# Log-sigmoid of the gates spread over 128 partitions, sums of x built on POOL from high and low parts

## The chip, the cores and the metric

The kernel runs on one core of one Trainium2 chip. Its time is the device time of one execution in microseconds (us). A core has a matrix engine (PE, with its weight load PEld), a vector engine (DVE), a scalar engine (ACT), a fourth engine for general work (POOL), a sequencer that issues transfers (SP), and DMA engines that move data between the chip's main memory and the on-chip memory, SBUF. PE writes its results to PSUM, from which DVE and ACT read. In the trace's names, `SPq` and `POOLq` are the transfers that SP and POOL issue.

## The reference

One inference step of a one-layer decoder: 512 prompt tokens and 8 x 4 sample tokens, 544 rows in all, each of 2048 numbers. All rows go through one large input projection; the mLSTM branch and the sliding-window attention branch work on its columns, and two further projections and an output projection follow. What matters here is the start:

```python
u = jnp.einsum('btd,dc->btc', x, w_in)      # 2048 inputs, 18,952 columns
...
q_m, k_m, v_m, o_m, z_m, q_a, k_a, v_a, z_a, g_m, g_a, i_pre, f_pre = parts
...
ig = (i_pre + b_igate).astype(jnp.float32)
lf = jax.nn.log_sigmoid((f_pre + b_fgate).astype(jnp.float32))
```

There are 4 heads, so `i_pre` and `f_pre` have 4 columns each. The mLSTM takes running sums of `lf` and running maxima of `ig` less those sums along the tokens of each head. Everything else of the mLSTM (decays, weights, stabilisers) is computed from these. The products are held in near-f32 accuracy.

## The kernel before

**Splitting.** PE multiplies a reduced-precision type (`fp32r` in the trace). Each f32 operand is therefore split into a high part (ACT: a copy that rounds; for weights L200, CAST in the trace) and a low part (DVE: the original less the high part; for weights L201). A product is three matmuls: high by high, high by low, low by high. `hilo` (L243 on ACT, L244 on DVE) does this for data.

**The x stage** (L287 to L346). x is loaded in columns, PE transposes it in blocks of 128 into a PSUM tile `pt` (`sm` in the trace), and for each of 16 blocks `hilo` writes high and low parts. For blocks 0 to 7 the first 272 rows of x go to `a11` and the rest to `a21`; blocks 8 to 15 go to `xk2`. ACT also copies the transposed x in f32 into `n2r` (L327) and `s1r` (L328, L338). From these, sums and differences are made: DVE subtracts in `s1r` (L332, L342), POOL adds `n3r = n2r + s1r` in four chunks of 128 x 544 (L346) when block 7 is in place, POOL subtracts in `n2r` later (`x_sums`), and high and low parts of the sums (`n3`, `s1`, `n2`, `s4`) are written by ACT and DVE (L565 for `n3l`, L244 for the others).

**The products.** The first two 128-column blocks are plain products, with the gate products (`gates_half`) between. After that, pairs of 128-column blocks go through `paired`: seven half-size products per pair in place of eight, from sums of the weights' quarters and sums of x's quarters (one level of a Strassen-type scheme). `prepare` makes the weights' sums, on DVE (L644) or, where an operand accumulates in place, as a transfer that adds (L642, issued by POOL's queue), and splits them. `half_product` (L664 and L666) issues the matmuls. `gather` combines the results: ACT evacuates (L682), POOL subtracts (L683), DVE does the rest (L685 to L693). The gathered blocks and other results pass through a pool of three buffers, `ev`.

**What runs beside.** The vector work of the gates, of the keys and of the values is written as generators (`gates`, `attn_values`, `attn_keys`, `x_sums`) that are advanced one step at a time: the products call `tick()`, and each `yield` ends a step. So the place of an instruction in DVE's order is set by the number of `yield`s ahead of it, together with a scheduler that respects priorities (`high_priority`). On each engine the order is fixed when the program is built.

`gates` first joins the four PSUM pieces of the gate products to `ig` and `fg`, of 4 partitions (the heads) by 544 tokens (L403 to L410). Then come, all on 4 partitions: the absolute value and the exponential on ACT (L414, L415), and on DVE `2 + e`, a reciprocal (L420), two multiplications (L424, L425), a polynomial (L427 to L432, with seven coefficients) and the joining of the minimum (L433, L434): `lf = min(f, 0) - log(1 + exp(-|f|))`, by a series. Fills (L438 to L440, L445 to L447) make the reset masks for two scans (L441: the running sum; L451: the running maximum). Rows of 4 x 544 live in a pool `t544` of 12 buffers.

`attn_values` copies 32 sample rows of the values into a buffer `vs` taken from `ev` (L533, L535) and stores it. `attn_keys` (L548 to L551) copies keys to a buffer `kr` taken from `ev`, and stores them in two transfers.

SP issues the weight loads (512 KB each), the stores of results and the small loads in program order.

Of the kernel before, what the change touches and what calls it, by code (L numbers as in the profile page):

```python
# [17 lines left out]
AF = mybir.ActivationFunctionType  # L18
ALU = mybir.AluOpType

D = 2048
SEQ = 512
NB = 8
NTS = 4
NS = NB * NTS
T = SEQ + NS
# [42 lines left out]
def build(tc, nc, i, o, dbg=None):  # L69
    es = ExitStack()  # L70
    with es:
        _build(tc, nc, i, o, es)


def _build(tc, nc, i, o, es):
# [3 lines left out]
    def pool(stack, name, bufs, space=None, side=None):  # L79
        kw = {"space": space} if space is not None else {}  # L80
        if space is None:
            kw["side"] = side or "right"
            kw["reuse_waits"] = "tile"
        return stack.enter_context(tc.tile_pool(name=name, bufs=bufs, **kw))

    y_p, y_s, C_p, n_p, m_p, kb_p, vb_p, C_s, n_s, m_s, kb_s, vb_s = o
    V, A, G, PE = nc.vector, nc.scalar, nc.gpsimd, nc.tensor
# [13 lines left out]
    def nm(s):  # L101
        count[0] += 1
        return f"{s}_{count[0]}"

    def sm():
        return psB.tile([128, 512], F32, tag="sm", name=nm("sm"))

    def ev(n=T):
        return evp.tile([128, n], F32, tag="ev", name=nm("ev"))

    def r32(ap):
        return ap.bitcast(F32)
# [4 lines left out]
    def blk(ap, n=4):  # L117
        return ap.rearrange("p (b x) -> p b x", b=n)
# [123 lines left out]
    def hilo(src, hi, lo, eng=None):  # L242
        A.copy(hi, src)  # L243
        (eng or V).tensor_tensor(out=lo, in0=src, in1=r32(hi), op=ALU.subtract)  # L244
# [10 lines left out]
    HT = T // 2  # L255

    def quad(p, s):
        return [p.tile([128, 8, HT], F32R, tag="act", name=nm(s + n)) for n in "hl"]

    a11, a21 = quad(act, "a11"), quad(act, "a21")  # L260
# [16 lines left out]
    esG = ExitStack()  # L277
# [5 lines left out]
    n2r = tx.tile([128, 8, HT], F32, name="n2r")[:]  # L283
    s1r, n3r = (act2.tile([128, 8, HT], F32, tag="act", name=nm("r"))[:] for _ in range(2))

    def two_k(ch):
        return slice(ch * 2, ch * 2 + 2)  # L287
# [11 lines left out]
    for c0, n in ((0, 256), (256, 256), (512, 512), (1024, 512), (1536, 512)):  # L299
        if c0 < 1536:  # L300
            t_ = xr.tile([128, 4, n], F32, tag=f"x{n}", name=nm("xr"))[:]
        else:
            t_ = act2.tile([128, 8, HT], F32, tag="act", name=nm("xr"))[:].rearrange("p a b -> p (a b)")
            t_ = blk(t_[:, 0:4 * n])
# [10 lines left out]
    for g in range(8):  # L315
        for q in range(2):
            k = g * 2 + q
            pt = sm()
            for t in range(4):
                PE.transpose(pt[:, t * 128:t * 128 + 128], xt[k][:, t], ident)  # L320
            if k == 2:
                for c in range(4):
                    PE.transpose(pxs[:, c * 128:c * 128 + 128], xs[:, c], ident)
            if k < 8:
                hilo(pt[:, 0:HT], a11[0][:, k], a11[1][:, k])
                hilo(pt[:, HT:SEQ], a21[0][:, k, 0:SEQ - HT], a21[1][:, k, 0:SEQ - HT])
                A.copy(n2r[:, k], pt[:, 0:HT])  # L327
                A.copy(s1r[:, k, 0:SEQ - HT], pt[:, HT:SEQ])  # L328
            else:
                hilo(pt[:], xk2[0][k // 4 - 2][:, k % 4, 0:SEQ], xk2[1][k // 4 - 2][:, k % 4, 0:SEQ])  # L330
                c = (slice(None), k - 8, slice(0, SEQ - HT))
                state["x_end"] = V.tensor_tensor(out=s1r[c], in0=pt[:, HT:SEQ], in1=s1r[c], op=ALU.subtract)  # L332
        if g % 2:
            k4 = slice((g // 2) * 4, (g // 2) * 4 + 4)
            src = pxs[:].rearrange("p (c q t) -> p q c t", c=4, q=4)[:, g // 2]
            if g < 4:
                hilo(src, *(a21[p][:, k4, SEQ - HT:HT] for p in range(2)))
                A.copy(s1r[:, k4, SEQ - HT:HT], src)  # L338
            else:
                hilo(src, *(xk2[p][g // 2 - 2][:, :, SEQ:T] for p in range(2)))  # L340
                c = (slice(None), slice(k4.start - 8, k4.stop - 8), slice(SEQ - HT, HT))
                V.tensor_tensor(out=s1r[c], in0=src, in1=s1r[c], op=ALU.subtract)  # L342
        if g == 3:
            for ch in range(4):
                ks_ = two_k(ch)
                G.tensor_tensor(out=n3r[:, ks_], in0=n2r[:, ks_], in1=s1r[:, ks_], op=ALU.add)  # L346
    esXr.close()
    t544 = pool(esG, "t544", 12)

    def t5(dt=F32, n=T):  # L350
        return t544.tile([128, n], dt, tag="t544", name=nm("t"))
# [41 lines left out]
    def gates(ps):  # L393
        def row(n=T):
            return t5(n=n)[:4]
# [5 lines left out]
            return ap.unsqueeze(2).to_broadcast([4, NB, NTS])  # L401

        ig, fg, u, u2 = row(), row(), row(), row()  # L403
        for p_, (u_, v_), (ig_, fg_) in zip(ps, *(
                [(a[:, c:c + HT], b[:, c:c + HT]) for c in (0, HT)] for a, b in ((u, u2), (ig, fg)))):
            A.copy(u_, p_[64:68, :HT])
            A.copy(v_, p_[96:100, :HT])
            V.scalar_tensor_tensor(ig_, p_[0:4, :HT], bi[:, 0:1], u_, op0=ALU.add, op1=ALU.add)
            V.scalar_tensor_tensor(fg_, p_[32:36, :HT], 0.0, v_, op0=ALU.add, op1=ALU.add)
        V.tensor_scalar(fg, fg, bi[:, 1:2], None, op0=ALU.add)  # L410
        yield
        e_ = row()
        A.activation(e_, fg, AF.Abs)
        A.activation(e_, e_, AF.Exp, scale=-1.0)  # L414
        yield  # L415
        yield

        dd, s, s2, p, lf = row(), u, u2, row(), row()
        V.tensor_scalar(dd, e_, 2.0, None, op0=ALU.add)
        V.reciprocal(dd, dd)  # L420
        yield
        yield
        yield
        V.tensor_tensor(out=s, in0=e_, in1=dd, op=ALU.mult)  # L424
        V.tensor_tensor(out=s2, in0=s, in1=s, op=ALU.mult)  # L425
        yield
        V.tensor_scalar(p, s2, 1.0 / 15, None, op0=ALU.mult)  # L427
        for c in (13, 11, 9, 7, 5, 3):
            V.scalar_tensor_tensor(p, p, 1.0 / c, s2, op0=ALU.add, op1=ALU.mult)
            if c % 4 == 1:  # L430
                yield
        V.scalar_tensor_tensor(p, p, 1.0, s, op0=ALU.add, op1=ALU.mult)  # L432
        V.tensor_scalar(lf, fg, 0.0, None, op0=ALU.min)  # L433
        V.scalar_tensor_tensor(lf, p, -2.0, lf, op0=ALU.mult, op1=ALU.add)  # L434
        yield

        rst, c = s, s2
        V.memset(rst, 1.0)  # L438
        V.memset(rst[:, 0:SEQ:128], 0.0)
        V.memset(rst[:, SEQ:T:NTS], 0.0)  # L440
        V.tensor_tensor_scan(c, rst, lf, 0.0, ALU.mult, ALU.add)  # L441
        ap, d0 = lf, row()
        V.tensor_tensor(out=ap, in0=ig, in1=c, op=ALU.subtract)
        yield
        V.memset(d0, 0.0)  # L445
        V.tensor_copy(d0[:, 128:SEQ:128], c[:, 127:SEQ - 1:128])
        V.memset(d0[:, SEQ:T:NTS], NEG)  # L447
        am, M = p, fg
# [58 lines left out]
        for src, rep, dst, m in ((T2, reps[0], colT2, 3), (T1, reps[1], colT1, 4)):  # L507
            pt, pt2 = sm(), sm()
# [15 lines left out]
    def attn_values(kk, vt):  # L524

        for _ in range(3):
            yield
        pt, pt2 = sm(), sm()
        for b in range(4):
            PE.transpose(pt[:, b * 128:b * 128 + 128], vt[:, b * 128:b * 128 + 128], ident)  # L530
        PE.transpose(pt2[:32, 0:128], vt[:, SEQ:T], ident)
        cs = slice(kk * 128, kk * 128 + 128)
        vr, vs = ev(512), ev(128)  # L533
        A.copy(vr[:], pt[:])
        V.tensor_copy(vs[:32], pt2[:32, 0:128])  # L535
        nc.sync.dma_start(d_vr[0:SEQ, cs].rearrange("(b p) c -> p b c", p=128), blk(vr[:]))
        nc.sync.dma_start(d_vr[SEQ:T, cs], vs[:32])
        nc.sync.dma_start(vb_p[0].rearrange("t k d -> t (k d)")[:, cs], vr[:, 384:512])
# [777 lines left out]
    for part, h in ((oz, 0), (oz, 1), (vkq, 2), (vkq, 3), (oz, 2), (oz, 3)):  # L1316
        work += part(h)
    work += merge_gates[7:]
    gates_ = gates(gates_ps)
    next(gates_)  # L1320
    spawn(gates_)
# [6 lines left out]
    def branch(src, p, tmp, ahead=()):  # L1328

        hs, los = act_tiles(p, "bh"), act_tiles(p, "bl")  # L1330

        def steps():
            for k in range(KT):
                if k < len(ahead):
                    st = ahead[k]
                else:
                    st = tmp(k)
                    nc.sync.dma_start(st[:], src[k])
                hilo(st[:], hs[k // 4][:, k % 4], los[k // 4][:, k % 4])
                yield  # L1340
        return (hs, los), whole(hs), whole(los), steps()

    _, bah, bal, g_ = branch(d_bra, act, lambda k: ev(), ahead)
# [12 lines left out]
    t544 = pool(esA, "t512", 18)  # L1356
# [289 lines left out]
    d0 = pool(esD, "d0", 1, side="left")  # L1646
# [248 lines left out]
```

## Time and profile before

| | |
|---|---|
| median of 3 runs | 2493.77 us (2491.63 to 2494.89) |
| profiled execution: its own time | 2497.55 us |
| its span (first to last instruction) | 2495.7 us |
| mean granted TensorE clock | 0.995 |
| PE busy in the span | 2453.8 us (98%) |
| DVE, ACT, POOL busy | 73%, 50%, 15% |
| costliest groups off PE | L201 on DVE 778.9 us, L200 on ACT 661.9 us, L644 on DVE 304.5 us |
| POOL's largest group | L683, 82 instructions, 124.8 us, 1522 ns each |

The profiled execution is one run, with the profiler on; the three timed runs have none. The traced times are read against the span of that execution, and differences worked out from them are then set against the median. A row of the timeline gives the start and the duration in us, the engine, the line of the kernel, the operation, output and inputs with partitions x elements, and in brackets the idle time just before with what ended it. Neighbouring instructions can overlap a little, since the start of one is put down before the end of the one ahead. A row of the groups gives busy time and mean duration in ns, then the idle time before the group.

### The profile page before, as it was taken

How to read it: one execution, taken by the hardware profiler on the slowest of the kernel's cores; microseconds unless marked ns; L12 is line 12 of the kernel's file. 1: busy time of each engine (PE TensorE's matmuls, PEld its weight loads, DVE VectorE, ACT ScalarE, POOL GpSimd, SP SyncE). 2: the span in 40 equal slices, each digit the busy share in tenths (PEclk: the TensorE clock that was granted, in tenths of full speed). 3: DMA queues.
4: the chain of work that ended last, by engine and by line, in shares of the span. 5: the costliest groups of instructions: out<-in, count | busy, mean ns of one | idle time of the engine just before them, and what ended most of it. 6: DMA issues, size and time to landing. Idle time of an engine off the chain costs nothing. (4 is left out here: it accounts for less than half of the span.)

```text
span 2495.7 us, 48772 instructions
## 1 busy us (share of the span) xinstructions
PE 2453.8 (98%) x19542; PEld 2394.0 (96%) x19542; DVE 1817.8 (73%) x2785; ACT 1244.1 (50%) x2033; POOL 373.1 (15%) x376
## 2 busy tenths in 40 slices
PE   8999999999999999999999999999999999999997
PEld 8999999999999999989999999999999999999997
DVE  7867677677677677777878788878855654666667
ACT  6457677667667665433433444444633333334431
POOL 2111121121111111121021121210000000110111
PEclk9999999999999999999999999999999999999999
DMA  6677666656666655468678677677755546788776
GB/s 166 154 185 187 150 151 159 158 144 163 153 152 156 151 128 151 106 204 243 205 216 243 167 232 240 188 225 226 251 171 172 189 149 205 198 229 258 213 220 190
DMA packets 557172, 464.71 MB, mean 186 GB/s; under 512 B 45328, under 2 KB 454080, under 8 KB 556688
## 3 DMA queue, kind: packets, MB, share of 16 engines
q1 hardware_dynamic: 540048, 402.07, 54.4%
q0 software_dynamic: 15696, 57.15, 11.8%
q8 instruction: 154, 2.52, 0.4%
q10 hardware_dynamic: 1200, 2.36, 0.3%
q14 instruction: 74, 0.61, 0.1%
HBM read 319.06 MB, written 96.31 MB: 166 GB/s over the span
## 5 line engine op out<-in xcount | busy, mean ns | idle before, releaser
L200 ACT CAST wh<-raw 128x1024 fp32r<-128x1024 f32 x632 | 661.9, 1048 | 814.6 <-PE bank L664 663.8
L201 DVE TENSOR_TENSOR wl<-raw,wh 128x1024 fp32r<-128x1024 f32 x632 | 778.9, 1234 | 222.7 <-ACT wh L200 203.4
L664 PE MATMUL bank<-xk,wh 128*128 128x272 f32 x2336 | 325.0, 290 | 0.9 <-DVE ev L689 0.9
L644 DVE TENSOR_TENSOR raw<-raw,raw 128x1024 f32<-128x1024 f32 x238 | 304.5, 1280 | 17.3 <-DMA raw<-in_w_in 8.2
L664 PEld LDWEIGHTS bank<-xk,wh 128*128 128x128 f32 x2336 | 304.3, 189 | 4.2 <-issue 2.6
L683 POOL TENSOR_TENSOR ev<-p,ev 128x272 f32<-128x272 f32 x82 | 124.8, 1522 | 674.1 <-ACT ev L682 613.7
L666 PE MATMUL bank<-xk,wl 128*128 128x272 f32 x1168 | 172.4, 288 | 0.8 <-DVE wl L201 0.8
L664 PE MATMUL bank<-s1h,wh 128*128 128x272 f32 x656 | 169.1, 291 | 0.2 <-ACT wh L200 0.2
L664 PE MATMUL bank<-n3h,wh 128*128 128x272 f32 x656 | 169.1, 289 | 0.0
L664 PE MATMUL bank<-n2h,wh 128*128 128x272 f32 x656 | 168.2, 289 | 0.6 <-ACT wh L200 0.6
L664 PE MATMUL bank<-s4h,wh 128*128 128x272 f32 x656 | 168.3, 290 | 0.1
L664 PE MATMUL bank<-n3l,wh 128*128 128x272 f32 x656 | 167.9, 287 | 0.0
L664 PE MATMUL bank<-n2l,wh 128*128 128x272 f32 x656 | 167.5, 287 | 0.0
L664 PE MATMUL bank<-s1l,wh 128*128 128x272 f32 x656 | 167.2, 287 | 0.0
L664 PE MATMUL bank<-s4l,wh 128*128 128x272 f32 x656 | 167.0, 287 | 0.0
L666 PEld LDWEIGHTS bank<-xk,wl 128*128 128x128 f32 x1168 | 156.6, 188 | 1.1 <-DVE wl L201 1.0
L664 PE MATMUL bank<-a11h,wh 128*128 128x272 f32 x584 | 150.8, 290 | 2.6 <-ACT wh L200 2.5
L209 PE MATMUL bank<-bh,wl 128*128 128x272 f32 x704 | 148.5, 291 | 4.7 <-DVE wl L201 4.7
L664 PE MATMUL bank<-a11l,wh 128*128 128x272 f32 x584 | 149.6, 289 | 0.0
L209 PE MATMUL bank<-bh,wh 128*128 128x272 f32 x704 | 148.8, 290 | 0.0
L209 PE MATMUL bank<-bl,wh 128*128 128x272 f32 x704 | 148.6, 290 | 0.0
L664 PEld LDWEIGHTS bank<-n3h,wh 128*128 128x128 f32 x656 | 123.3, 188 | 1.9 <-issue 1.4
(488 smaller groups left out, 5515.4 us busy)
## 6 DMA issues: line engine op xcount, KB each, us to landing
raw<-in_w_in SPq DMA_DIRECT2D x296, 512.0 KB
raw<-raw POOLq DMA_DIRECT2D x90, 512.0 KB, 5.0
C<-in_state_mlstm_C SPq DMA_DIRECT2D x32, 1024.0 KB
out<-C SPq DMA_DIRECT2D x64, 512.0 KB
raw<-in_w_proj_a SPq DMA_DIRECT2D x32, 512.0 KB
raw<-in_w_proj_m SPq DMA_DIRECT2D x32, 512.0 KB
raw<-in_w_out SPq DMA_DIRECT2D x32, 512.0 KB
d_v<-ev SPq DMA_DIRECT2D x16, 272.0 KB
```

The source lines that it names most:

```text
L200: A.copy(wh[:, k:k + n], raw[:, k:k + n])
L201: V.tensor_tensor(out=wl[:, k:k + n], in0=raw[:, k:k + n], in1=r32(wh[:, k:k + n]), op=ALU.subtract)
L209: PE.matmul(ps[f][:, :w], a[:, kk], b(k, c, w), start=(k == 0 and n == 0), stop=(k == 15 and n == 2))
L644: V.tensor_tensor(out=w[out][:], in0=w[a][:], in1=w[b][:], op=ALU.add)
L664: PE.matmul(ps, wh[:, k], x(p, k), start=(first and k == 0 and p == 0), stop=False, skip_group_check=True)
L666: state["end"] = PE.matmul(ps, wl[:, k], x(0, k), start=False, stop=(k == 7), skip_group_check=True)
L683: G.tensor_tensor(out=c22, in0=p1, in1=c11, op=ALU.subtract)
```

## The change

Three parts.

1. **Sums of x.** ACT no longer copies the transposed x into `n2r` and `s1r` (18 copies fall away). POOL adds high and low parts instead: when blocks 0 to 3, and again when blocks 4 to 7, are in place, two chunks of 128 x 544 each for `s1r` (from `a21`) and for `n2r` (from `a11`). That is eight POOL additions more, ahead of the four for `n3r`.
2. **Log-sigmoid.** `fg` is moved by a transfer from 4 partitions of 544 to 128 partitions of 17 (`f7`, a slice of one new buffer `w7`); ACT's two steps and DVE's fourteen run on 128 x 17, and a second transfer brings the result back to `lf`, 4 x 544. Both transfers are issued by SP. The same arithmetic is done. The large fills of the scans' masks (`rst`, `d0`) go to POOL; one strided copy and one fill for the second scan stay on DVE. There are fewer `yield`s. `t544` has 13 buffers.
3. **`vs`** comes from `t544` in place of `ev`.

```diff
--- before.py
+++ after.py
@@ -324,8 +324,6 @@
             if k < 8:
                 hilo(pt[:, 0:HT], a11[0][:, k], a11[1][:, k])
                 hilo(pt[:, HT:SEQ], a21[0][:, k, 0:SEQ - HT], a21[1][:, k, 0:SEQ - HT])
-                A.copy(n2r[:, k], pt[:, 0:HT])
-                A.copy(s1r[:, k, 0:SEQ - HT], pt[:, HT:SEQ])
             else:
                 hilo(pt[:], xk2[0][k // 4 - 2][:, k % 4, 0:SEQ], xk2[1][k // 4 - 2][:, k % 4, 0:SEQ])
                 c = (slice(None), k - 8, slice(0, SEQ - HT))
@@ -335,7 +333,10 @@
             src = pxs[:].rearrange("p (c q t) -> p q c t", c=4, q=4)[:, g // 2]
             if g < 4:
                 hilo(src, *(a21[p][:, k4, SEQ - HT:HT] for p in range(2)))
-                A.copy(s1r[:, k4, SEQ - HT:HT], src)
+                for t_, (h_, l_) in ((s1r, a21), (n2r, a11)):
+                    for ch in (g - 1, g):
+                        ks_ = two_k(ch)
+                        G.tensor_tensor(out=t_[:, ks_], in0=r32(h_[:, ks_]), in1=r32(l_[:, ks_]), op=ALU.add)
             else:
                 hilo(src, *(xk2[p][g // 2 - 2][:, :, SEQ:T] for p in range(2)))
                 c = (slice(None), slice(k4.start - 8, k4.stop - 8), slice(SEQ - HT, HT))
@@ -345,7 +346,7 @@
                 ks_ = two_k(ch)
                 G.tensor_tensor(out=n3r[:, ks_], in0=n2r[:, ks_], in1=s1r[:, ks_], op=ALU.add)
     esXr.close()
-    t544 = pool(esG, "t544", 12)
+    t544 = pool(esG, "t544", 13)
 
     def t5(dt=F32, n=T):
         return t544.tile([128, n], dt, tag="t544", name=nm("t"))
@@ -401,6 +402,7 @@
             return ap.unsqueeze(2).to_broadcast([4, NB, NTS])
 
         ig, fg, u, u2 = row(), row(), row(), row()
+        w7 = t5(n=6 * 17)
         for p_, (u_, v_), (ig_, fg_) in zip(ps, *(
                 [(a[:, c:c + HT], b[:, c:c + HT]) for c in (0, HT)] for a, b in ((u, u2), (ig, fg)))):
             A.copy(u_, p_[64:68, :HT])
@@ -408,41 +410,38 @@
             V.scalar_tensor_tensor(ig_, p_[0:4, :HT], bi[:, 0:1], u_, op0=ALU.add, op1=ALU.add)
             V.scalar_tensor_tensor(fg_, p_[32:36, :HT], 0.0, v_, op0=ALU.add, op1=ALU.add)
         V.tensor_scalar(fg, fg, bi[:, 1:2], None, op0=ALU.add)
-        yield
-        e_ = row()
-        A.activation(e_, fg, AF.Abs)
-        A.activation(e_, e_, AF.Exp, scale=-1.0)
-        yield
-        yield
-
-        dd, s, s2, p, lf = row(), u, u2, row(), row()
-        V.tensor_scalar(dd, e_, 2.0, None, op0=ALU.add)
-        V.reciprocal(dd, dd)
-        yield
-        yield
-        yield
-        V.tensor_tensor(out=s, in0=e_, in1=dd, op=ALU.mult)
-        V.tensor_tensor(out=s2, in0=s, in1=s, op=ALU.mult)
-        yield
-        V.tensor_scalar(p, s2, 1.0 / 15, None, op0=ALU.mult)
-        for c in (13, 11, 9, 7, 5, 3):
-            V.scalar_tensor_tensor(p, p, 1.0 / c, s2, op0=ALU.add, op1=ALU.mult)
-            if c % 4 == 1:
-                yield
-        V.scalar_tensor_tensor(p, p, 1.0, s, op0=ALU.add, op1=ALU.mult)
-        V.tensor_scalar(lf, fg, 0.0, None, op0=ALU.min)
-        V.scalar_tensor_tensor(lf, p, -2.0, lf, op0=ALU.mult, op1=ALU.add)
-        yield
-
-        rst, c = s, s2
-        V.memset(rst, 1.0)
-        V.memset(rst[:, 0:SEQ:128], 0.0)
-        V.memset(rst[:, SEQ:T:NTS], 0.0)
+        e_, dd, p, lf, d0 = (row() for _ in range(5))
+        rst, c = u, u2
+        G.memset(d0, 0.0)
+        f7, e7, d7, s7, q7, p7 = (w7[:, n * 17:n * 17 + 17] for n in range(6))
+        nc.sync.dma_start(f7, fg)
+        yield
+        yield
+        A.activation(e7, f7, AF.Abs)
+        A.activation(e7, e7, AF.Exp, scale=-1.0)
+        yield
+
+        V.tensor_scalar(d7, e7, 2.0, None, op0=ALU.add)
+        V.reciprocal(d7, d7)
+        V.tensor_tensor(out=s7, in0=e7, in1=d7, op=ALU.mult)
+        V.tensor_tensor(out=q7, in0=s7, in1=s7, op=ALU.mult)
+        V.tensor_scalar(p7, q7, 1.0 / 15, None, op0=ALU.mult)
+        for n in (13, 11, 9, 7, 5, 3):
+            V.scalar_tensor_tensor(p7, p7, 1.0 / n, q7, op0=ALU.add, op1=ALU.mult)
+        V.scalar_tensor_tensor(p7, p7, 1.0, s7, op0=ALU.add, op1=ALU.mult)
+        V.tensor_scalar(f7, f7, 0.0, None, op0=ALU.min)
+        V.scalar_tensor_tensor(f7, p7, -2.0, f7, op0=ALU.mult, op1=ALU.add)
+        nc.sync.dma_start(lf, f7)
+        G.memset(rst, 1.0)
+        G.memset(rst[:, 0:SEQ:128], 0.0)
+        G.memset(rst[:, SEQ:T:NTS], 0.0)
+        yield
+        yield
+
         V.tensor_tensor_scan(c, rst, lf, 0.0, ALU.mult, ALU.add)
-        ap, d0 = lf, row()
+        ap = lf
         V.tensor_tensor(out=ap, in0=ig, in1=c, op=ALU.subtract)
         yield
-        V.memset(d0, 0.0)
         V.tensor_copy(d0[:, 128:SEQ:128], c[:, 127:SEQ - 1:128])
         V.memset(d0[:, SEQ:T:NTS], NEG)
         am, M = p, fg
@@ -530,7 +529,7 @@
             PE.transpose(pt[:, b * 128:b * 128 + 128], vt[:, b * 128:b * 128 + 128], ident)
         PE.transpose(pt2[:32, 0:128], vt[:, SEQ:T], ident)
         cs = slice(kk * 128, kk * 128 + 128)
-        vr, vs = ev(512), ev(128)
+        vr, vs = ev(512), t5(n=128)
         A.copy(vr[:], pt[:])
         V.tensor_copy(vs[:32], pt2[:32, 0:128])
         nc.sync.dma_start(d_vr[0:SEQ, cs].rearrange("(b p) c -> p b c", p=128), blk(vr[:]))
```

## The prediction

> **What bounds the kernel now.** I read the page first, then stretches of 25 us, then the PE, DVE, ACT, POOL and SP timelines of the first 105 us. The built programs order every engine's instructions alike behind about 150 us, so only the start can differ.
>
> ```profile
> PE 2453.8 (98%) x19542; PEld 2394.0 (96%) x19542; DVE 1817.8 (73%) x2785; ACT 1244.1 (50%) x2033; POOL 373.1 (15%) x376
> ```
> ```profile
> 25.00:50.00 25.00, 23.20 (x183) 22.53 (x184) 22.42 (x40) 15.25 (x36) 10.77 (x9) 1.00 0.42 96
> 50.00:75.00 25.00, 24.20 (x194) 23.97 (x193) 24.02 (x30) 13.52 (x22) 6.74 (x5) 1.00 0.51 111
> 75.00:100.00 25.00, 23.00 (x178) 22.10 (x177) 21.80 (x37) 8.29 (x10) 3.30 (x3) 1.00 0.70 182
> 100.00:125.00 25.00, 23.31 (x185) 23.00 (x183) 19.72 (x36) 13.59 (x19) 2.43 (x3) 1.00 0.70 163
> ...
> 150.00:175.00 25.00, 25.00 (x201) 25.00 (x201) 15.88 (x19) 13.24 (x18) 3.11 (x3) 1.00 0.81 196
> ```
> Columns of the stretches are the length, then PE, weight load, DVE, ACT and POOL busy. PE is the bound. From 150 us it never rests (201 matmuls in 25 us, 0.125 us each); before that it rests while DVE is all but full, 24.02 of 25 us. Most that the change can win is PE rest ahead of 105 us. The rests that matter, with the start of the first weight pair's products (57.79) for a mark:
>
> ```profile
> 57.79 0.29 PE L664 MATMUL bank<-a11h,wh 128*128 128x272 f32 x1
> ...
> 69.77 1.27 PE L666 MATMUL bank<-xk,wl 128*128 128x272 f32 x8 [0.80 <-DVE wl L201]
> ...
> 78.42 0.39 PE L664 MATMUL bank<-a11h,wh 128*128 128x272 f32 x1 [0.84 <-ACT wh L200]
> ...
> 81.55 2.27 PE L664 MATMUL bank<-xk,wh 128*128 128x272 f32 x16 [0.86 <-DVE ev L689]
> ...
> 85.96 0.39 PE L664 MATMUL bank<-s1h,wh 128*128 128x272 f32 x1 [0.16 <-ACT wh L200]
> ...
> 103.78 0.39 PE L664 MATMUL bank<-a11h,wh 128*128 128x272 f32 x1 [1.69 <-ACT wh L200]
> ```
> They add up to 0.80 + 0.84 + 0.86 + 0.16 + 1.69 = 4.35 us. A gain over 0.2% (5 us, about what a measurement of this kernel can tell from no change) therefore needs the stage of the x transposes, ahead of 57.79, as well.
>
> **The log-sigmoid.** The old chain works on 4 partitions of 544 elements, so each step costs its full length:
>
> ```profile
> L429 DVE SCALAR_TENSOR_TENSOR t<-t,t 4x544 f32<-4x544 f32 x6 | 4.2, 695 | 0.0
> L420 DVE RECIPROCAL t<-t 4x544 f32<-4x544 f32 x1 | 3.5, 3541 | 0.0
> ...
> L425 DVE TENSOR_TENSOR t<-t 4x544 f32<-4x544 f32 x1 | 0.7, 706 | 0.0
> ...
> L438 DVE MEMSET t<- 4x544 f32 x1 | 0.5, 512 | 0.1
> ...
> L535 DVE COPY ev<-sm 32x128 f32<-32x128 f32 x1 | 0.3, 279 | 2.8 <-DMA out<-ev 2.8
> ...
> L450 DVE TENSOR_TENSOR t<-t,m0t 4x8 f32<-4x8 f32 x1 | 0.2, 153 | 0.0
> ```
> Removed from DVE: the reciprocal 3.5, six polynomial steps 4.2, four more two-input steps like L425 (L424, L432, L434) 4 x 0.7 = 2.8, the long fills L438 and L445 1.0, and three one-input steps I put at 0.4 each, 1.2: 12.7 us. In their place are fourteen steps on 128 partitions of 17. Nothing in the trace has that shape; nearest is the 0.15 us row of 8 elements, so 14 x 0.15 = 2.1 us (above by the 32-column steps, not much more). DVE wins some 10.6 us. Keeping the small value copy out of the `ev` buffers also removes the 2.8 us for which DVE stood behind a store. That DVE time is worth only what PE waited for, and what comes late next is a chain that runs through POOL and transfers:
>
> ```profile
> 66.48 3.85 POOL L683 TENSOR_TENSOR ev<-p,ev 128x272 f32<-128x272 f32 x1 [10.39 <-ACT ev L682]
> 70.29 0.86 POOL L642 DMA_DIRECT2D raw<-raw  x1
> ...
> 94.61 1.64 POOL L683 TENSOR_TENSOR ev<-p,ev 128x272 f32<-128x272 f32 x1 [8.72 <-DMA out<-ev]
> 96.21 0.86 POOL L642 DMA_DIRECT2D raw<-raw  x1
> ```
> ```profile
> 76.38 1.99 ACT L200 CAST wh<-raw 128x1024 fp32r<-128x1024 f32 x2 [4.17 <-DVE t L447]
> ...
> 101.74 1.99 ACT L200 CAST wh<-raw 128x1024 fp32r<-128x1024 f32 x2 [5.05 <-DMA raw<-raw]
> ```
> ```profile
> 90.33 0.27 DVE L548 COPY ev<-sm 128x128 f32<-128x128 f32 x1
> ```
> ```profile
> 91.06 0.38 SPq L551 DMA_DIRECT2D d_ks<-ev  x1
> ```
> ```profile
> 61.03 0.49 DVE L410 TENSOR_SCALAR t<-t,bi 4x544 f32<-4x544 f32 x1
> ```
> Read it forward: POOL's subtraction (L683), POOL's accumulating transfer at 70.29, the cast at 76.38 (6.1 us on), DVE's work up to the key copy at 90.33, its store from 91.06 on, POOL's next subtraction that reuses that buffer at 94.61 (3.2 us after the store was issued at 91.44), the transfer at 96.21, the two casts at 101.74, PE at 103.78. In the changed program these links remain:
> (i) Start. The gates are complete at 61.5 (L410 at 61.03). The transfer out is issued by SP in 0.4, lands after 3.2 (from the 91.44 to 94.61 above; the other bound is 6.1, the accumulating transfer), two ACT steps take 0.4, then ACT's queued cast 1.0 and evacuation 0.4, POOL 1.64: 68.6 instead of 70.29, 1.7 us earlier. POOL's 3.85 falls to the 1.64 of its later row, since the 3.5 us reciprocal, on DVE at the same time, is gone. ACT stands on this transfer with the casts of the later products queued behind; PE wants the first of them some 12 us after it starts the pair, which covers it up to a landing of about 7 us.
> (ii) DVE from the cast to the key copy: the second scan and its sums now stand there instead of the polynomial, while the 2.8 us wait is gone. I add the instructions in the new order, 13.3 us behind the first cast's 1.0, against the 13.95 between 76.38 and 90.33 that held both casts: 0.4 later by that count, or 0.6 earlier when the cast is taken inside; I take 0.6 earlier and keep both. The transfer back lands during the weight subtraction ahead of the scan, so costs nothing; without that cover it costs what it exceeds 1.2 us.
> (iii) PE's first product behind the last transfer is now that of the first cast, not the second: 1.0 us earlier.
> Sum: -(1.7 + 0.6 + 1.0) = -3.3 us. PE alone could come 4.35 earlier, so the chain decides; a wait of about 1 us stays near 100 us. SP's issue of the outward transfer also holds back the next weight load, which waits until 62.68 for DVE anyway.
>
> ```profile
> 62.68 0.38 SPq L635 DMA_DIRECT2D raw<-in_w_in  x1
> ```
>
> **The sums of x.** ACT loses eighteen copies; POOL takes eight additions more.
>
> ```profile
> L327 ACT COPY n2r<-sm 128x272 f32<-128x272 f32 x8 | 3.4, 427 | 0.2 <-DVE a21l L244 0.2
> L328 ACT COPY r<-sm 128x240 f32<-128x240 f32 x8 | 3.3, 410 | 0.0
> ```
> ```profile
> L244 DVE TENSOR_TENSOR xk<-sm,xk 128x512 fp32r<-128x512 f32 x6 | 4.1, 680 | 0.8 <-ACT xk L243 0.8
> ...
> L244 DVE TENSOR_TENSOR a11l<-sm,a11h 128x272 fp32r<-128x272 f32 x7 | 3.0, 437 | 3.5 <-ACT a11h L243 3.5
> ```
> ```profile
> L346 POOL TENSOR_TENSOR r<-n2r,r x4: 1338/1354/1842, 14.9 to 28.9; 128x544 f32<-128x544 f32 x4
> ```
> The copies stood in front of the casts that DVE waited for, 3.5 + 0.8 = 4.3 us; I take all of it back. Against it: DVE steps with two inputs in SBUF stop while a POOL addition runs.
>
> ```profile
> 18.82 0.72 DVE L565 SCALAR_TENSOR_TENSOR n3l<-r,n3h 128x544 fp32r<-128x544 f32 x1
> ...
> 23.70 1.16 DVE L565 SCALAR_TENSOR_TENSOR n3l<-r,n3h 128x544 fp32r<-128x544 f32 x1
> ...
> 29.68 1.96 DVE L385 TENSOR_TENSOR wga<-graw,wga 128x32 fp32r<-128x32 f32 x2
> ...
> 40.22 3.79 DVE L244 TENSOR_TENSOR s1l<-r,s1h 128x544 fp32r<-128x544 f32 x4
> ...
> 47.29 0.29 DVE L385 TENSOR_TENSOR wga<-graw,wga 128x32 fp32r<-128x32 f32 x2
> ```
> ```profile
> 28.92 1.36 POOL L346 TENSOR_TENSOR r<-n2r,r 128x544 f32<-128x544 f32 x1
> ```
> The two `wga` steps take 1.96 beside additions and 0.29 without; with 0.4 + 0.2 on two of the four n3l steps and 1.1 on the s1l steps, DVE pays 3.4 us over these ten steps now, 0.34 each, with eight additions. With sixteen, back to back from about 13 us, twelve such steps fall among them; at twice the density w = 0.68 each, which is also half an addition, that is 8.2 us. Net: 8.2 - 3.4 - 4.3 = +0.5 us, which PE pays at the end of the transposes, since in the new order it has no gate products left to fill in there. The Trainium skill's "SBUF — State Buffer", section "Who interferes with whom", speaks against the change here: a DVE instruction with two SBUF inputs and a GpSimd instruction that reads SBUF exclude each other for the whole instruction. Read at its worst, every step would wait one addition whole, 12 x 1.35 - 7.7 = +8.5, and the sum would be +5.2 instead of -2.8; the 1.96 beside the 28.92 POOL row shows the exclusion, and the 0.72 row that not every step meets it.
>
> ```profile
> 28.00 0.97 POOL L379 MEMSET wgb<- 128x1024 f32 x1
> ```
> The fills on POOL go into its idle time (15% busy), at most 1 us each by the 0.97 row, ahead of buffers that DVE needs later. Bounded below by no gain, above by 1 us.
>
> **Sum.** -3.3 + 0.5 = -2.8 us against the profiled 2497.55 (its span 2495.7 and 1.85 around it): 2494.7. The median of the runs shown is 2493.77, 3.8 below the profiled one; I forecast on that scale, 2493.77 - 2.8 = 2491.0.
>
> **Rivals.** With w as the mean wait of the twelve steps, the total is -3.3 - 7.7 + 12w.
> *Faster by more than 0.2%*: w under 0.50. For it: the 0.34 of today, and DVE finds POOL waiting for it as often. Against it: twice the additions. At 0.34 the sum is -6.9, 2486.9. Chance 0.38, since ACT's relief may also shorten PE's smaller gaps that I left alone.
> *Slower*: POOL becomes the bound of the x stage. Its sixteen additions and two fills (the 0.97 row) take 16 x 1.35 + 2 x 0.97 = 23.5 us, and whatever DVE blocks is added; the sums, the second gate weights and the high and low parts all queue behind. It decides above w = 1.33, a whole addition. With additions stretched towards the 1.84 of the longest row, w = 1.5 gives +7.0, 2500.8. For it: the pair at 29.68 came close to 0.84 each. Chance 0.14.
> *The transfers take the place of the arithmetic*: the first lands after 6.1 instead of 3.2, moving link (i) by 2.9: +0.1, 2493.9, no measurable change. Both transfers queue on SP behind 512 KB loads, which speaks for it; chance 0.18, of which 0.06 for landings so late that ACT's casts hold PE (slower).
> The forecast itself, w between 0.50 and 1.33 with prompt transfers: 0.30.
>
> **How the numbers follow.** Within 0.2%: 0.30 + 0.12 = 0.42. Faster: 0.38. Slower: 0.14 + 0.06 = 0.20. The likeliest case's own range is 2488.8 to 2498.8; the range for all runs from w = 0.2 (-8.6, 2485) to the slower rival's near part, 2500.
>
> **What would show it.** Right: no PE rest between 58 and 95 us, one of 1 to 2 us near 100 us behind an ACT cast; POOL at its subtraction in about 1.6 us; DVE's 17-element steps near 0.15; n3l, wga and wl steps over 1.2 us beside POOL additions between 13 and 42 us, and the start of the first pair's products near 58. Wrong: that start before 55 or after 62, an ACT idle above 3 us ahead of the absolute value, a scan waiting for the transfer back, or any difference that opens behind 150 us.

## The result, and the profile after

Over 22 runs of each kernel the changed one takes 2486.77 us (median; 2482.05 to 2494.10) and the one before 2490.85 us. The ratio is 0.9982, with a 95% interval of 0.9976 to 0.9988: 4.5 us faster, between 3.0 and 6.0. That is 0.18%, just on the near side of the 0.2% drawn as a line in the prediction. (The median of before over 22 runs lies 2.9 us under that of the first three.)

The profiled execution took 2484.96 us, its span is 2483.2 us. Its engines, as in the first section of the page:

```profile
PE 2447.4 (99%) x19542; PEld 2390.9 (96%) x19542; DVE 1811.9 (73%) x2781; ACT 1238.8 (50%) x2015; POOL 385.1 (16%) x388
```

The stretches of 25 us (length, then PE, weight load, DVE, ACT, POOL busy, then the granted clock):

```profile
25.00:50.00 25.00, 22.72 (x179) 21.95 (x178) 22.74 (x39) 14.29 (x32) 15.87 (x13) 1.00 0.47 116
50.00:75.00 25.00, 25.00 (x203) 24.99 (x202) 20.90 (x39) 14.24 (x23) 3.90 (x6) 1.00 0.60 142
75.00:100.00 25.00, 23.38 (x183) 22.72 (x183) 23.30 (x44) 11.93 (x18) 4.16 (x5) 1.00 0.68 169
100.00:125.00 25.00, 25.00 (x203) 24.85 (x202) 17.03 (x23) 10.16 (x14) 3.95 (x4) 1.00 0.86 216
```

PE no longer rests from 50 to 75 and from 100 to 125 us, where it had 24.20 and 23.31 of 25. Its rests, from the timeline, with the start of the first pair's products:

```profile
22.52 0.63 PE L320 MATMUL sm<-cc,xr 128*128 128x128 f32 x4 [2.72 <-DVE a21l L244]
...
46.19 0.48 PE L391 MATMUL bank<-xk,wga 128*128 128x272 f32 x2 [2.28 <-DVE wga L386]
...
56.26 0.29 PE L663 MATMUL bank<-a11h,wh 128*128 128x272 f32 x1
...
80.85 1.27 PE L665 MATMUL bank<-a11h,wl 128*128 128x272 f32 x8 [0.84 <-DVE wl L201]
...
90.83 1.27 PE L665 MATMUL bank<-xk,wl 128*128 128x272 f32 x8 [0.30 <-DVE wl L201]
...
92.58 0.36 PE L663 MATMUL bank<-n3h,wh 128*128 128x272 f32 x1 [0.48 <-DVE ev L684]
```

Behind the first pair's start the rests fall from 4.35 to 0.84 + 0.30 + 0.48 = 1.62 us. The start itself is 1.53 us earlier, but that is not the change. From 13.5 to 16.9 us the run of before had a granted clock of 0.50, the run after 1.00 (third column from the end; first the row of before, then that of after):

```profile
13.50:16.90 3.40, 3.40 (x16) 3.40 (x17) 1.44 (x5) 2.62 (x11) 1.34 (x1) 0.50 1.12 333
```
```profile
13.50:16.90 3.40, 3.40 (x31) 3.40 (x30) 2.49 (x8) 2.29 (x8) 3.40 (x4) 1.00 1.13 336
```

In the traces of the table below such stretches last 3.4 or 6.8 us, apart from one that takes up the last 11 to 14 us of each, and they lie elsewhere in other executions. The Trainium skill, "TensorE: Matmul & The Clock Gate", section "What's actually happening", gives the gate a free-running window of 3.4 us, and the lengths agree. The two spans differ by 12.5 us, three times the timed difference: by the 1501st matmul (near 202 us) PE is 5.7 us ahead, and most of the rest opens between 1890 and 2280 us, in work that the change does not touch. Near 2150 us PE rested 4.02 us in the run of before, with 6.8 us of half clock; in the run after it rested 0.63 us there, with none.

So parts are compared below in two ways: timed, in 5 rounds, good to some 2.5 us; and by PE's position in the trace, from matmul 361, which starts 1.37 us behind the first pair's start in every run, to matmul 1501. The clock was full there in every run of the table.

| kernel | first pair's start, us | half clock ahead of it, us | from matmul 361 to 1501, us | timed ratio (95%) |
|---|---|---|---|---|
| before | 57.79 | 3.4 at 13.5 | 148.6 | 1 |
| changed | 56.26 | none | 144.4 | 0.9982 (0.9976 to 0.9988) |
| sums of x alone | 58.04 | 3.4 at 22.6 | 149.0 | 1.0003 (0.9990 to 1.0015) |
| value copy's buffer alone | 58.14 | 3.4 at 13.6 | 146.3 | 0.9986 (0.9976 to 0.9997) |
| log-sigmoid alone | 57.52 | 3.4 at 13.2 | 145.8 | 0.9982 (0.9971 to 0.9993) |
| log-sigmoid and buffer | 55.86 | none | 144.8 | 0.9975 (0.9966 to 0.9984) |
| changed, additions and copies both | 61.33 | 6.8 at 42.2 | 144.9 | 1.0001 (0.9992 to 1.0010) |
| changed, small additions | 59.44 | 3.4 at 41.2 | 145.6 | 0.9992 (0.9980 to 1.0004) |
| changed, return on POOL | 58.10 | 3.4 at 22.4 | 143.3 | 0.9983 (0.9973 to 0.9993) |
| changed, rows of 4 | 56.41 | none | 149.0 | 0.9990 (0.9980 to 0.9999) |
| no sums, return on POOL | 58.18 | 3.4 at 13.5 | 143.4 | 0.9978 (0.9966 to 0.9989) |
| changed, out by main memory | 56.70 | none | 145.4 | 0.9980 (0.9970 to 0.9990) |

### The profile page after: what moved, and what is told of

The parts are those of the page before. It is cut to its first block, busy times and chain, and to the rows that moved or that the text cites. A ratio compares the mean times of both kernels' runs of the same rounds, so it can differ in the third digit from the quotient of the medians.

```text
span 2483.2 us, 48768 instructions
## 1 busy us (share of the span) xinstructions
PE 2447.4 (99%) x19542; PEld 2390.9 (96%) x19542; DVE 1811.9 (73%) x2781; ACT 1238.8 (50%) x2015; POOL 385.1 (16%) x388
## 4 chain that ended last, share of the span: by engine, by line
PE 89%; issue 4%; DMA 3%; DVE 3%; ACT 1%; SPq 0%; POOL 0%; DVEq 0%; ACTq 0%; POOLq 0%
PE bank L663 44%; PE bank L665 22%; PE bank L209 9%; PE sm L1398 2%; PE sm L1430 1%; PE bank L1210 1%; PE sm L771 1%; PE sm L1443 1%; PE sm L809 1%; PE sm L799 1%; DMA raw<-in_w_in 1%; PE sm L209 1%; PE sm L1760 1%; DVE wl L201 1%; DMA VB<-d_kv 1%
```

## The experiments

**The parts.** Four kernels share their runs of before.

*Sums of x alone*, on the kernel before:

```diff
-                A.copy(n2r[:, k], pt[:, 0:HT])
-                A.copy(s1r[:, k, 0:SEQ - HT], pt[:, HT:SEQ])
...
-                A.copy(s1r[:, k4, SEQ - HT:HT], src)
+                for t_, (h_, l_) in ((s1r, a21), (n2r, a11)):
+                    for ch in (g - 1, g):
+                        ks_ = two_k(ch)
+                        G.tensor_tensor(out=t_[:, ks_], in0=r32(h_[:, ks_]), in1=r32(l_[:, ks_]), op=ALU.add)
```

> The kernel before with the sums of x alone (ACT's 18 copies out, POOL's eight additions in). Theory A (the prediction's steps): +0.5 us, between -3.6 (a mean wait w of 0.34 us for DVE's steps with two SBUF inputs) and +2.0; that is, all of the change's gain lies elsewhere. Theory B (the start of the first pair's products, 57.79 before and 56.26 after, is a real gain of this part): -1.5 us, products starting near 56.3, three of four n3l steps stretched to 1.4 to 1.9 us, and the later PE rests near 70, 78, 82, 86 and 104 us unchanged in sum (4.35). Theory C (the half-clock stretch that the profiled run before had at 13.5 to 16.9 us made that difference): no change, products starting near 57.8 less the dip's share, so within 0.5 us of a run of before without it.

2492.51 us against 2492.70: no change that can be told, as theories A and C have it. The timing alone does not exclude theory B's 1.5 us, but the trace does: with a half-clock stretch of 3.4 us in each, the start is 0.25 us later than in the run of before, not earlier.

*Value copy's buffer alone*: `vs` from `t544` (13 buffers).

```diff
-        vr, vs = ev(512), ev(128)
+        vr, vs = ev(512), t5(n=128)
```

> The kernel before with the small value copy in a buffer of its own (t544 of 13) in place of the ev pool, nothing else. The DVE wait of 2.8 us behind a store goes. Theory A (the chain through POOL and the key store decides): the key copies come up to 2.8 us earlier, so the PE rest of 1.69 us near 104 shrinks and the time falls by 0.5 to 1.7 us. Rival (DVE's arithmetic of the log-sigmoid decides; the wait is swallowed by the steps that queue behind): no change within 0.5 us.

2489.49 us, ratio 0.9986, and 2.3 us in the trace: more than the 1.7 of theory A's upper end. The later of the two POOL subtractions moves ahead of 94.61, and the rest of 1.69 us on the second transfer is gone; so is that of 0.86 us near 82 us, while one of 0.77 us near 108 us is new:

```profile
92.49 0.78 POOL L683 TENSOR_TENSOR ev<-p,ev 128x272 f32<-128x272 f32 x1 [8.63 <-DMA d_ks<-ev]
```

*Log-sigmoid alone*: the changed kernel with ACT's copies and `vs` from `ev`, as before.

> The kernel after without the sums of x and with the small value copy in the ev pool again: the spread log-sigmoid alone. Theory A: most of the product stage's gain stays, -2 to -3 us, since 12.7 us of DVE steps become about 3; the PE rests between 60 and 100 us fall from 4.35 to below 2 us. Rival (the ev buffer decides): the 2.8 us wait of the copy stays, the POOL subtraction near 92 us is late and the time falls by no more than 1 us.

2488.59 us, ratio 0.9982, and 2.8 us in the trace: theory A. The copy, queued elsewhere now, does not stand behind a store, although it is back in `ev`.

*Log-sigmoid and buffer*: the changed kernel with ACT's copies in place of POOL's additions.

> The kernel after without the sums of x: log-sigmoid and value copy together. Theory A (on record): -3.3 us. Theory B (from the two traces: rests of PE of 4.35 us become 1.62, and 1.5 come from the sums of x): -2.7 us. If the parts add up, this run and that of the sums of x alone add up to the -4.1 to -4.5 us of the whole change; a sum far from that means that one part's gain depends on the other.

2487.20 us, ratio 0.9975, and 3.8 us in the trace. The two parts alone make 2.3 + 2.8 = 5.1: they share 1.3 us, since both shorten the one chain to POOL's second subtraction. It comes 36.8 us behind the first pair's start before, and 34.3 to 34.4 with either part alone or with both. This run and the changed one have the clock full throughout the x stage, so their starts can be set side by side:

```profile
55.86 0.29 PE L662 MATMUL bank<-a11h,wh 128*128 128x272 f32 x1
```

55.86 without the sums of x, 56.26 with them: the sums cost 0.40 us there. At matmul 1501 it is 0.05, since the longer rest without them (1.17 us instead of 0.84 near 81 us) takes it back:

```profile
80.78 1.27 PE L664 MATMUL bank<-a11h,wl 128*128 128x272 f32 x8 [1.17 <-DVE wl L201]
```

**The two sides of the sums.** *Additions and copies both*: the changed kernel with ACT's 18 copies put back ahead of the additions.

```diff
                 hilo(pt[:, HT:SEQ], a21[0][:, k, 0:SEQ - HT], a21[1][:, k, 0:SEQ - HT])
+                A.copy(n2r[:, k], pt[:, 0:HT])
+                A.copy(s1r[:, k, 0:SEQ - HT], pt[:, HT:SEQ])
...
+                A.copy(s1r[:, k4, SEQ - HT:HT], src)
```

> The changed kernel with ACT's 18 copies put back ahead of POOL's additions, which write the same tiles again: POOL's additions without ACT's relief. Theory A (the prediction's steps: relief of ACT is worth 4.3 us, the additions cost DVE 8.2 less 3.4): the first pair's products start some 4 us later than the 56.3 of the changed kernel, near 60.5, and the time is within 0.5 us of the kernel before. Rival (ACT has slack and its copies cost nothing, and the additions cost nothing either): products start within 0.5 us of 56.3 and the time stays 4 to 5 us under the kernel before.

2491.97 us, ratio 1.0001 (0.9992 to 1.0010): the gain is gone, as theory A has it. In the trace the start is at 61.33 with 6.8 us of half clock from 42 us on, so some 57.9 without, 1.7 us late instead of 4. The direction is shown, the size is not. The copies also changed the order on POOL, and DVE now stood behind one of its additions:

```profile
36.77 0.72 DVE L332 TENSOR_TENSOR r<-sm,r 128x240 f32<-128x240 f32 x2 [3.09 <-POOL r L350]
```

*Small additions*: each new addition writes 128 x 16 elements in place of 128 x 544, and two POOL fills at the start (not shown) put a constant in the rest. The kernel leaves the sums of x out, and keeps ACT's relief.

```diff
-                        ks_ = two_k(ch)
-                        G.tensor_tensor(out=t_[:, ks_], in0=r32(h_[:, ks_]), in1=r32(l_[:, ks_]), op=ALU.add)
+                        ks_ = (slice(None), two_k(ch), slice(HT - 8, HT))
+                        G.tensor_tensor(out=t_[ks_], in0=r32(h_[ks_]), in1=r32(l_[ks_]), op=ALU.add)
```

> The changed kernel with each of the eight new POOL additions cut to the last 8 of 272 columns (128 x 16 in place of 128 x 544); the other columns of the sums hold a constant written by POOL at the start, so the sums of x are left out. ACT's relief without POOL's work. Theory A: the eight additions cost 8.2 - 3.4 = 4.8 us by the prediction's w of 0.68, or about 2.5 by the stretch seen on the changed kernel (n3l, wl and s1l steps 5.1 us over their undisturbed time, of which half is due to the new additions); products start 2.5 to 4.8 us before 56.3. Rival (PE's transposes and products set the stage whatever DVE does): within 0.5 us of 56.3, and the same time as the changed kernel.

2491.22 us, ratio 0.9992 (0.9980 to 1.0004): not faster than the changed kernel, rather slower, so theory A's time misses. The scheduler put most of the second plain product ahead of the gates' second half, PE and DVE waited for each other, and PE's start came no earlier (59.44, with 3.4 us of half clock ahead of it). What it does show is DVE's own progress. Its last step for the sums, from the timelines of log-sigmoid and buffer, of the changed kernel, and of this one:

```profile
42.17 2.63 DVE L244 TENSOR_TENSOR n2l<-n2r,n2h 128x544 fp32r<-128x544 f32 x4
```
```profile
45.12 0.72 DVE L244 TENSOR_TENSOR n2l<-n2r,n2h 128x544 fp32r<-128x544 f32 x1
```
```profile
37.34 2.63 DVE L244 TENSOR_TENSOR n2l<-n2r,n2h 128x544 fp32r<-128x544 f32 x4
```

They end at 44.80, 45.84 and 39.97: with neither ACT's copies nor long additions DVE is there 4.8 and 5.9 us earlier. But not all of this is the price of copies and additions, since one `wl` step that stands ahead of this point in the other two orders stands behind it here (first log-sigmoid and buffer, then this run):

```profile
35.31 1.23 DVE L201 TENSOR_TENSOR wl<-raw,wh 128x1024 fp32r<-128x1024 f32 x1 [1.67 <-ACT wh L200]
```
```profile
39.89 1.22 DVE L201 TENSOR_TENSOR wl<-raw,wh 128x1024 fp32r<-128x1024 f32 x1
```

From its start to that of the next step it takes 1.14 us, and 2.81 with the wait ahead of it. In the changed kernel a step on `n2r` of 0.64 us has moved ahead as well. Less these, ACT's copies cost DVE 2.0 to 3.7 us, and the additions 2.4 to 4.1.

*Side by side*: the lock by itself, on scratch, ahead of x.

```diff
+    V.memset(s1r[:, 0:4], 1.0)
+    for _ in range(8):
+        G.memset(n2r[:, 0:2], 1.0)
+    for _ in range(3):
+        V.tensor_tensor(out=n3r[:, 2:4], in0=s1r[:, 0:2], in1=s1r[:, 2:4], op=ALU.add)
+        V.tensor_scalar(n3r[:, 4:6], s1r[:, 0:2], 2.0, None, op0=ALU.add)
+    for _ in range(8):
+        G.tensor_tensor(out=n3r[:, 0:2], in0=n2r[:, 0:2], in1=n2r[:, 0:2], op=ALU.add)
+    for _ in range(5):
...
```

> The kernel before with work added on scratch at its start, ahead of x: POOL fills (128 x 544) and then eight additions of that shape, and beside them on DVE by turns additions with two SBUF inputs (0.71 us alone in the traces so far) and steps with one input, both 128 x 544. Only durations are read. Theory A (a two-input DVE step and a POOL addition exclude each other): beside the additions the two-input steps take up to 0.71 + 1.36 us, the single-input steps keep their length, and beside the fills neither is stretched; some POOL additions are stretched by a DVE step. Rival (bandwidth of SBUF shared by all): all DVE steps beside additions are stretched alike, and less than twofold.

POOL fills until 6.52 us and adds from 6.60 us on. DVE's rows, and POOL's eight additions:

```profile
4.56 0.71 DVE L295 TENSOR_TENSOR r<-r 128x544 f32<-128x544 f32 x1
5.19 0.84 DVE L296 TENSOR_SCALAR r<-r 128x544 f32<-128x544 f32 x1
5.95 0.70 DVE L300 TENSOR_TENSOR r<-r 128x544 f32<-128x544 f32 x1
6.58 0.43 DVE L301 TENSOR_SCALAR r<-r 128x544 f32<-128x544 f32 x1
6.93 1.61 DVE L300 TENSOR_TENSOR r<-r 128x544 f32<-128x544 f32 x1
8.47 1.33 DVE L301 TENSOR_SCALAR r<-r 128x544 f32<-128x544 f32 x1
9.72 1.61 DVE L300 TENSOR_TENSOR r<-r 128x544 f32<-128x544 f32 x1
...
14.03 0.43 DVE L244 TENSOR_TENSOR a11l<-sm,a11h 128x272 fp32r<-128x272 f32 x1
```
```profile
6.60 11.74 POOL L298 TENSOR_TENSOR r<-n2r 128x544 f32<-128x544 f32 x8
```

Theory A holds for two inputs (0.71 becomes 1.61 beside additions, stays 0.71 beside fills) and fails for one: 0.43 becomes 1.33 beside additions (0.98 once, in a row left out above) and up to 0.84 beside fills. Both kinds pay 0.90 us; a step that reads PSUM keeps its 0.43. An addition takes 11.74 / 8 = 1.47 instead of 1.36.

**The chain and its transfers.** *Return on POOL's queue*:

```diff
-        nc.sync.dma_start(lf, f7)
+        G.dma_start(out=lf, in_=f7)
```

> The changed kernel with the transfer that brings the log-sigmoid back to 4 rows issued by POOL's queue in place of SP's; PE, DVE and ACT orders all but unchanged. In the changed kernel it was issued at 73.37, 3 us after DVE had its data (70.35), behind two weight loads and a store on SP, and the scan waited 2.33 us for it until 76.12. Theory A (SP's queue holds it): it is issued within 1 us of 70.4, the scan starts by 74, and the PE rests of 0.84 near 81 and 0.48 near 92.6 shrink: 0.5 to 1.3 us faster than the changed kernel. Rival (the landing itself is slow, or POOL's queue takes longer): the scan waits as long, and the time is the same.

In the changed kernel DVE's result is there at 70.35. SP was in the second of two weight loads, which waited 3.0 us for a buffer that POOL's accumulating transfer still used (the row of 3.81 us below holds both loads and this wait; the second was issued at 71.40). A store came next, and the scan waited. Below, the first row is from the view of waits (total, times, longest):

```profile
70.17 0.18 DVE L433 SCALAR_TENSOR_TENSOR t<-t 128x17 f32<-128x17 f32 x1
```
```profile
SPq L187 <- DMA raw<-raw: 3.0, 1, 3.0
```
```profile
67.96 3.81 SPq L187 DMA_DIRECT2D raw<-in_w_in  x2
71.86 1.42 SPq L535 DMA_DIRECT2D d_vr<-ev  x1
73.37 0.62 SPq L434 DMA_DIRECT2D t<-t  x1
```
```profile
76.12 1.28 DVE L441 TENSOR_TENSOR_SCAN t<-t,t 4x544 f32<-4x544 f32 x1 [2.33 <-DMA t<-t]
```

With the return on POOL (its start is 1.84 us later throughout, by the half clock):

```profile
72.50 0.76 POOL L434 DMA_DIRECT2D t<-t  x1 [3.52 <-DVE t L534]
```
```profile
76.81 1.28 DVE L441 TENSOR_TENSOR_SCAN t<-t,t 4x544 f32<-4x544 f32 x1 [1.19 <-DMA t<-t]
```

It is issued 0.3 us after the data, the wait is halved, and PE gains 1.1 us (143.3 for 144.4) as theory A has it. The rival is partly right too: from the start of the issue to the scan it takes 4.3 us there and 2.75 by SP, so of 2.7 us won at the issue the scan keeps 1.15. Why the landing is slower is not shown. The timed ratio, 0.9983, cannot tell 1.1 us.

*Rows of 4*: the same order and fills, no transfers.

```diff
-        f7, e7, d7, s7, q7, p7 = (w7[:, n * 17:n * 17 + 17] for n in range(6))
-        nc.sync.dma_start(f7, fg)
+        f7, e7, d7, s7, q7, p7 = fg, e_, dd, dd, w7[:4], p
...
-        nc.sync.dma_start(lf, f7)
```

> The changed kernel with the log-sigmoid computed on 4 x 544 again, in the new order (few yields, fills on POOL, the value copy in its own buffer), no transfers. Theory A (the shape of the arithmetic pays): about 10 us of DVE come back, of which the value copy's own buffer recovers none; the PE rests between 60 and 100 us rise again to 3 to 4 us and the time is 1 to 2.5 us over the changed kernel. Rival (the order, the fills and the buffer pay, not the shape): within 0.5 us of the changed kernel, since the 2.33 us wait for the transfer goes as well. A third outcome, more than 4 us over it, would say that the undivided chain stalls DVE's weight steps more than the spread-out one before did.

In the trace 4.6 us over the changed kernel, the third outcome; timed, 2488.92 us, about 2 us over it, which is theory A's range. Either way the shape pays. The long reciprocal is back, POOL's subtraction beside it, and the rest on the second transfer:

```profile
63.72 3.54 DVE L424 RECIPROCAL t<-t 4x544 f32<-4x544 f32 x1
```
```profile
65.10 3.86 POOL L680 TENSOR_TENSOR ev<-p,ev 128x272 f32<-128x272 f32 x1 [8.05 <-ACT ev L679]
```
```profile
101.64 0.40 PE L661 MATMUL bank<-a11h,wh 128*128 128x272 f32 x1 [2.38 <-ACT wh L200]
```

*Out by main memory*:

```diff
-        nc.sync.dma_start(f7, fg)
+        d_f = dr.tile([4, T], F32, name="d_f")
+        nc.sync.dma_start(d_f[:], fg)
+        nc.sync.dma_start(f7, d_f[:].rearrange("h (a t) -> (h a) t", t=17))
```

> The changed kernel with the outward transfer of the gates by way of main memory, in two transfers: it lands later, by 2 us or more. ACT stands on it with a cast and the evacuation that POOL's subtraction needs queued behind. Theory A (the prediction's link (i): POOL's subtraction and transfer and all that follows move by the same amount, covered for PE's casts up to a landing of about 7 us): POOL's subtraction at 64.95 moves to 67 or later, and the time rises by 1 to 2.5 us over the changed kernel. Rival (there is room behind it, as for the 2.33 us wait of the scan, of which PE paid about 1.1): less than 1 us.

Inconclusive for link (i): the scheduler moved the absolute value behind the evacuation on ACT, so POOL's subtraction came at 65.39, no later than the start's 0.44 us.

```profile
64.90 0.40 ACT L683 ACTIVATE ev<-bank 128x272 f32<-128x272 f32 x1
65.61 0.22 ACT L422 ACTIVATE t<-t 128x17 f32<-128x17 f32 x1 [0.30 <-DMA t<-d_f]
```

PE lost 1.0 us behind the start (145.4), through a scan that came 2.5 us later against it. Timed, 0.9980, no difference.

*No sums, return on POOL*: the version that the traces point to.

> The changed kernel without the sums of x and with the returning transfer on POOL's queue: the version that the traces point to. By the position of PE's matmuls, the sums of x cost 0.4 us at the first pair's start and the queue of SP 1.1 us behind it: from -1 us to -1.5 us against the changed kernel, that is, 5.1 to 6.0 us under the kernel before. Rival (what is won early is lost to a later wait, as the 0.4 us was by 95 us): the same time as the changed kernel, -4.1 to -4.5 us.

2487.47 us, ratio 0.9978. In the trace it is as quick behind the start as the other kernel with this return, 143.4. It beats the kernel before; against the changed kernel (0.9982) 5 rounds tell nothing, and neither theory is excluded.

## Why the prediction was right

The forecast was -2.8 us, within 0.2%; measured were -4.5 (-3.0 to -6.0), so the size forecast lies just outside the interval, and with 0.12 to 0.24% measured it is partly luck that the result fell on the near side of the 0.2% line. The parts came out as split: nearly nothing from the sums of x, the gain from the log-sigmoid and the value copy.

- **The sums, +0.5.** Measured +0.40 at the first pair's start, 0.05 in the end. The net holds, the terms are both smaller: small additions leave 2.0 to 3.7 us for ACT's relief, 4.3 forecast, and 2.4 to 4.1 for POOL's side, 4.8 forecast. And the mechanism is only part of it. The prediction put all of POOL's side on DVE's twelve two-input steps, 0.68 each. Their stretch on the changed kernel is less:

```profile
18.29 1.79 DVE L201 TENSOR_TENSOR wl<-raw,wh 128x1024 fp32r<-128x1024 f32 x1 [0.51 <-ACT wh L200]
20.01 1.85 DVE L564 SCALAR_TENSOR_TENSOR n3l<-r,n3h 128x544 fp32r<-128x544 f32 x1
...
26.16 1.43 DVE L564 SCALAR_TENSOR_TENSOR n3l<-r,n3h 128x544 fp32r<-128x544 f32 x1
...
34.51 1.59 DVE L201 TENSOR_TENSOR wl<-raw,wh 128x1024 fp32r<-128x1024 f32 x1 [1.94 <-ACT wh L200]
...
36.85 2.52 DVE L244 TENSOR_TENSOR s1l<-r,s1h 128x544 fp32r<-128x544 f32 x2
39.29 1.88 DVE L564 SCALAR_TENSOR_TENSOR n3l<-r,n3h 128x544 fp32r<-128x544 f32 x1
```

 Over 0.71 (n3l), 1.23 (wl) and 1.35 (the pair of s1l) that is 0.56 + 1.14 + 0.72 + 0.36 + 1.17 + 1.17 = 5.1 us, or w = 0.43. That is under the 0.50 of the faster rival, yet its -6.9 did not come: 5.1 - 3.4 = 1.7 us are new stretch, and the relief that stands against it was less than 4.3 as well. What the rest of POOL's side (0.7 to 2.4 us) consists of is open. That POOL's queue makes it up, which the prediction had only in its slower rival, is not shown: a fill for the gates' weights stood behind the additions, and ACT waited 1.11 us for it, but the next cast waited 0.69 us more for PE, which still read the weights it replaces, and DVE's `wl` at 34.51, which follows that cast, had waited 1.67 us without the additions too.

```profile
32.40 0.34 ACT L385 CAST wgb<-graw 128x32 fp32r<-128x32 f32 x2 [1.11 <-POOL wgb L380]
33.43 1.05 ACT L200 CAST wh<-raw 128x1024 fp32r<-128x1024 f32 x1 [0.69 <-PE bank L209]
```

- **Link (i), -1.7.** POOL's rows on the changed kernel, and the outward transfer with the step that waits for it:

```profile
64.95 1.38 POOL L682 TENSOR_TENSOR ev<-p,ev 128x272 f32<-128x272 f32 x1 [8.04 <-ACT ev L681]
66.27 0.87 POOL L641 DMA_DIRECT2D raw<-raw  x1
...
89.96 1.44 POOL L682 TENSOR_TENSOR ev<-p,ev 128x272 f32<-128x272 f32 x1 [9.24 <-DMA d_ks<-ev]
```
```profile
60.09 0.68 SPq L417 DMA_DIRECT2D t<-t  x1
```
```profile
62.55 0.22 ACT L420 ACTIVATE t<-t 128x17 f32<-128x17 f32 x1
```

 POOL's transfer went from 70.29 to 66.27; less the 1.53 of the start that is -2.5. POOL's 3.85 fell to 1.38. The outward transfer was issued at 60.09 and ACT's step began at 62.55, right behind a cast and without idle time, so the transfer took 2.5 us or less where 0.4 + 3.2 was put down.
- **Link (ii), -0.6: the step that failed.** The cast and the key copy:

```profile
71.48 1.05 ACT L200 CAST wh<-raw 128x1024 fp32r<-128x1024 f32 x1 [1.87 <-DMA raw<-raw]
```
```profile
86.82 0.25 DVE L547 COPY ev<-sm 128x128 f32<-128x128 f32 x1
```

 From the one to the other it took 15.3 us, not 13.95: +1.4. The return was said to cost nothing under the weight subtraction, and the bound (what exceeds 1.2 us) was taken as not met. The landing was prompt, but SP issued it 3.0 us late, behind the load that waited for POOL's transfer, so the scan waited 2.33 us. That both transfers queue on SP stood in a rival, but its price was worked out for the outward one alone. The return on POOL's queue shows what PE gains when part of that wait goes: 1.1 us. The miss of 2.0 us (-0.6 forecast, +1.4 measured) was covered by two terms that the prediction held fixed. From POOL's first transfer to the cast it took 5.2 us (66.27 to 71.48) instead of 6.1, and from the key copy to POOL's second subtraction 3.1 (86.82 to 89.96) instead of 4.3. With them this subtraction comes 3.1 us earlier against the start, where links (i) and (ii) make 2.3. That their sum was near is luck.
- **Link (iii), the rest near 100 us.** It did not come; PE's rests lie at 81 to 93 us and add up to 1.62. The key's buffer came free 2.4 us after the store's issue began at 87.53 (POOL at 89.96); counted alike it had been 3.5 (91.06 to 94.61).
- **The product stage, -3.3.** Without the sums it is 148.6 - 144.8 = 3.8 us in the trace. But the 4.35 was no upper bound: with the return on POOL the trace shows 148.6 - 143.3 = 5.3. The rests leave out what comes with them; the first matmul behind a rest takes 0.36 to 0.40 us where others take 0.29.
- **Fourteen steps at 0.15.** The six of the polynomial, from the groups by line:

```profile
L430 DVE SCALAR_TENSOR_TENSOR t<-t 128x17 f32<-128x17 f32 x6 | 1.6, 271 | 0.1
```

 With 0.27 for the reciprocal and 0.18 for each of the seven others they make 3.1 us where 2.1 was put down. What PE paid for it, no run shows.

## What to carry to other kernels

Before work is moved from ACT to POOL, price both of POOL's charges: DVE steps with all operands in SBUF can wait beside its additions, and whatever else is queued on POOL comes later to the engine that needs it (1.11 us for a fill, 3.09 for an addition, above). A short transfer inside a chain is as quick as the queue that issues it: look at what stands ahead of it there, at what that waits for in its turn, and at the engines whose queue is free; then compare the time to land as well. Where one execution's start is compared with another's, look at the granted clock of the stretch first.

## What was not expected of the hardware

A single-input DVE step with both ends in SBUF waits beside POOL's additions as a two-input one does, 0.90 us each, and is stretched beside fills too (0.43 to 0.84), where the two-input step is not. The Trainium skill, "SBUF — State Buffer", section "Who interferes with whom", has both kinds: two inputs against reads, and single-input steps in a fast mode against any use of the shared ports. These runs agree on who is held. They do not show the hold lasting for whole instructions: in the 2.79 us from one two-input step to the next (6.93 to 9.72) DVE did a step of each kind, 0.71 + 0.43 = 1.14 us alone, and POOL 2.79 / 1.47 = 1.9 additions, 2.6 us alone. That is 3.7 us of work, so a good part of it went side by side (POOL's records are rough).
